# Interleaving two arrays: 64 KiB store rows from one output buffer, one DMA queue in a fixed order

## The chip, the cores and the metric

The kernel runs on one NeuronCore of a Trainium2 chip. The metric is the device time of one execution in microseconds; lower is better. The core has 16 DMA engines that move data between HBM (the chip's main memory) and SBUF (the core's working memory, 128 partitions). A DMA is issued by an engine's queue (here those of SyncE, called SP in the profile, and of ScalarE, called ACT), and a DMA over 128 partitions puts 8 partition rows on each of the 16 DMA engines.

## What is computed

Two float32 arrays of 32 x 256 x 1024 elements are interleaved element by element:

```python
result = np.zeros((batch, seq, dim * 2), dtype=np.float32)
result[..., 0::2] = x
result[..., 1::2] = y
```

There is no arithmetic. The kernel reads 67.11 MB and writes 67.11 MB.

## The kernel before

All of `x` is seen as one flat run and cut into `n` = 8 tiles. A tile is 128 partitions x `W` = 8192 elements, 4 MiB, so a row of one partition is 32 KiB of HBM in one piece. `y` is cut in the same way. A tile of the output is 128 x 16384 elements, 8 MiB, 64 KiB for each partition.

SBUF holds six buffers of 32 KiB a partition: `xt[0]`, `xt[1]` for tiles of x, `yt[0]`, `yt[1]` for tiles of y, and `ot[0]`, `ot[1]` for the two halves of an output tile. Tile k uses `xt[k % 2]` and `yt[k % 2]`; half h of its output always goes through `ot[h]`.

Three engines run lists written out by hand, and semaphores order them:

- SyncE issues the loads (lines 37 to 48). The first half of x tile 0 comes first; ScalarE issues the other half at line 38, and both are moved ahead of the start barrier by `tile_interleave_kernel`. Then come y0, x1 and y1, which wait for nothing. From k = 2 on, the load of x tile k (line 45) waits until VectorE has counted `woven` up to the last copy that reads that `xt` buffer, and the load of y tile k (line 48) waits for one copy more.
- VectorE weaves (lines 50 to 63). For each tile and each half h it copies 4096 elements of x into the even elements of `ot[h]` (line 60) and then 4096 elements of y into the odd ones (line 63). Each copy adds 1 to `woven`. The x copy waits for x and, from the second tile on, until the store that last read `ot[h]` has landed (`osem[h]`, line 59). The first y copy of a tile waits for y.
- ScalarE issues the stores (lines 65 to 70): for each half, when its two copies are done, one DMA of 128 rows of 32 KiB, 64 KiB apart in HBM.

At the end ScalarE waits for all stores of `ot[0]` and clears the semaphores, and SyncE waits for the last store of `ot[1]`.

Of the kernel before, what the change touches and what calls it, by code (L numbers as in the profile page):

```python
# [3 lines left out]


def _interleave(nc, x, y, out):
    P = 128
    W = 8192
    H = W // 2  # L10

    total = 1
    for s in x.shape:
        total *= s
    n = total // (P * W)
    assert n * P * W == total

    def rows(ap, names, k):
        flat = ap.rearrange("b s d -> (b s d)")
        return flat[k * names : (k + 1) * names].rearrange("(p w) -> p w", p=P)  # L20

    fp32 = mybir.dt.float32
    xt = [nc.alloc_sbuf_tensor(f"xt{b}", [P, W], fp32).ap() for b in (0, 1)]
    yt = [nc.alloc_sbuf_tensor(f"yt{b}", [P, W], fp32).ap() for b in (0, 1)]
    ot = [nc.alloc_sbuf_tensor(f"ot{b}", [P, W], fp32).ap() for b in (0, 1)]

    xsem = [nc.alloc_semaphore(f"xsem{b}") for b in (0, 1)]
    hsem = nc.alloc_semaphore("hsem")
    ysem = [nc.alloc_semaphore(f"ysem{b}") for b in (0, 1)]
    woven = nc.alloc_semaphore("woven")  # L30
    osem = [nc.alloc_semaphore(f"osem{b}") for b in (0, 1)]

    xs = [rows(x, P * W, k) for k in range(n)]
    ys = [rows(y, P * W, k) for k in range(n)]
    os_ = [rows(out, 2 * P * W, k) for k in range(n)]

    nc.sync.dma_start(out=xt[0][:, :H], in_=xs[0][:, :H]).then_inc(xsem[0], 16)
    nc.scalar.dma_start(out=xt[0][:, H:], in_=xs[0][:, H:]).then_inc(hsem, 16)

    for k in range(n):  # L40
        b = k % 2
        if k >= 2:
            nc.sync.wait_ge(woven, 4 * (k - 2) + 3)
        if k:
            nc.sync.dma_start(out=xt[b], in_=xs[k]).then_inc(xsem[b], 16)
        if k >= 2:
            nc.sync.wait_ge(woven, 4 * (k - 2) + 4)
        nc.sync.dma_start(out=yt[b], in_=ys[k]).then_inc(ysem[b], 16)

    for k in range(n):  # L50
        b = k % 2
        for h in (0, 1):
            c = slice(h * H, (h + 1) * H)
            if h == 0:
                nc.vector.wait_ge(xsem[b], 16 * (k // 2 + 1))
            elif k == 0:
                nc.vector.wait_ge(hsem, 16)
            if k:
                nc.vector.wait_ge(osem[h], 16 * k)
            nc.vector.tensor_copy(out=ot[h][:, 0::2], in_=xt[b][:, c]).then_inc(woven, 1)  # L60
            if h == 0:
                nc.vector.wait_ge(ysem[b], 16 * (k // 2 + 1))
            nc.vector.tensor_copy(out=ot[h][:, 1::2], in_=yt[b][:, c]).then_inc(woven, 1)  # L63

    for k in range(n):
        for h in (0, 1):
            nc.scalar.wait_ge(woven, 4 * k + 2 * h + 2)
            nc.scalar.dma_start(
                out=os_[k][:, h * W : (h + 1) * W], in_=ot[h]
            ).then_inc(osem[h], 16)  # L70

    nc.scalar.wait_ge(osem[0], 16 * n)
    used = sorted(s.num for s in [*xsem, hsem, *ysem, woven, osem[0]])
    assert used == list(range(used[0], used[-1] + 1)), used
    nc.scalar.sem_clear(range(used[0], used[-1] + 1))
    nc.sync.nop(nofuse=True).wait_op(osem[1], 16 * n, "sem-ge").then_inc(
        osem[1], -16 * n
    )


def kernel(tc, x, y, out):
    nc = tc.nc
    tc.close()
    tc.compile()

    _interleave(nc, x, y, out)

    blocks = nc.main_func.blocks
    for engine in (mybir.EngineType.SP, mybir.EngineType.Activation):
        opening = blocks[0].instructions  # L90
        at, moved = next(
            (b, i)
            for b in blocks[1:]
            for i in b.instructions
            if i.engine == engine and i.opcode == "DMACopy"
        )
        assert not (moved.sync_info and moved.sync_info.on_wait)
        body = at.instructions
        body.remove(moved)
        gate = next(  # L100
            n
            for n, i in enumerate(opening)
            if i.engine == engine and i.opcode == "Drain"
        )
        opening.insert(gate, moved)
        at.instructions = body
        blocks[0].instructions = opening


# [1 line left out]
_INS = ['x', 'y']  # L111
_OUTS = [((32, 256, 2048), 'float32')]


# [23 lines left out]
```

## Time and profile before

| | us |
|---|---|
| median of 8 runs | 314.64 (314.48 to 314.90) |
| the profiled execution | 314.74 |
| its span, first to last instruction | 313.4 |
| VectorE busy in the span | 72.6 (23%), 32 copies |

The profile is one execution. Two rows of the page's table of groups tell what VectorE waits for. After the bar stand the busy time, the mean duration of one copy in ns, the idle time of the engine just before these copies, and what ended it:

```profile
L60 DVE COPY ot<-xt 128x4096 f32<-128x4096 f32 x16 | 36.7, 2295 | 183.2 <-DMA out_dram<-ot 171.5
L63 DVE COPY ot<-yt 128x4096 f32<-128x4096 f32 x16 | 36.7, 2291 | 42.8 <-DMA yt<-in_y_dram 42.8
```

The DMAs by the place where they are issued: the number of them, the size of one, and the median time from issue to landing:

```profile
out_dram<-ot ACTq DMA_DIRECT2D x16, 4096.0 KB, 29.0
yt<-in_y_dram SPq DMA_DIRECT2D x8, 4096.0 KB, 60.8
xt<-in_x_dram SPq DMA_DIRECT2D x7, 4096.0 KB, 43.6
xt<-in_x_dram SPq DMA_DIRECT2D x1, 2048.0 KB, 11.7
xt<-in_x_dram ACTq DMA_DIRECT2D x1, 2048.0 KB, 13.4
```

q1 in the profile is SyncE's DMA queue and q10 is ScalarE's. A packet is what a DMA engine records of one row, or of the small write to a semaphore with which each DMA ends on each engine.

### The profile page before, as it was taken

Reading aid. Unit: us, or ns where it says so; the run is one execution under the profiler, and the core shown is the slowest. Engines: PE = TensorE matmul, PEld = TensorE weight load, DVE = VectorE, ACT = ScalarE, POOL = GpSimd, SP = SyncE. Lnnn points to the kernel's source line nnn. Section 1 sums busy time; section 2 is a strip of 40 time slices with the busy share of each in tenths; the row PEclk is TensorE's granted clock in tenths of the full one; section 3 lists DMA queues with packets and bytes.
Section 4 is the critical chain, followed back from the end, with each engine's and each line's share of the span. In section 5 each row is a group of like instructions: output and inputs, shape, how many; then the busy total and the mean of one; then the engine's idle time right before and its main releaser. Section 6 shows DMA issues by size and latency. Waiting matters only on the chain.

```text
span 313.4 us, 113 instructions
## 1 busy us (share of the span) xinstructions
DVE 72.6 (23%) x32; POOL 0.2 (0%) x4
## 2 busy tenths in 40 slices
DVE  0216002232022410324103250031501315013510
POOL 0000000000000000000000000000000000000000
DMA  8999999999999999999999999999999999999998
GB/s 339 464 406 397 431 439 427 443 418 452 410 460 406 460 406 460 410 456 414 447 422 439 431 435 435 431 439 422 447 414 456 406 460 406 460 410 456 414 452 351
DMA packets 4752, 134.22 MB, mean 428 GB/s; under 512 B 528, under 2 KB 528, under 8 KB 528
## 3 DMA queue, kind: packets, MB, share of 16 engines
q10 hardware_dynamic: 2448, 69.21, 51.2%
q1 hardware_dynamic: 2304, 65.01, 48.5%
HBM read 67.11 MB, written 67.11 MB: 428 GB/s over the span
## 4 chain that ended last, share of the span: by engine, by line
DMA 82%; DVE 12%; issue 0%
DMA out_dram<-ot 76%; DMA yt<-in_y_dram 7%; DVE ot L63 6%; DVE ot L60 6%
## 5 line engine op out<-in xcount | busy, mean ns | idle before, releaser
L60 DVE COPY ot<-xt 128x4096 f32<-128x4096 f32 x16 | 36.7, 2295 | 183.2 <-DMA out_dram<-ot 171.5
L63 DVE COPY ot<-yt 128x4096 f32<-128x4096 f32 x16 | 36.7, 2291 | 42.8 <-DMA yt<-in_y_dram 42.8
L122 POOL MEMSET const-uint8-127<- 128x1 uint8 x1 | 0.1, 103 | 0.0
L122 POOL MEMSET const-bfloat16-1.0<- 128x1 bf16 x1 | 0.1, 102 | 0.0
L122 POOL MEMSET const-float32-0.0<- 128x1 f32 x1 | 0.1, 99 | 0.2 <-issue 0.2
L122 POOL MEMSET const-float32-1.0<- 128x1 f32 x1 | 0.1, 99 | 0.0
## 6 DMA issues: line engine op xcount, KB each, us to landing
out_dram<-ot ACTq DMA_DIRECT2D x16, 4096.0 KB, 29.0
yt<-in_y_dram SPq DMA_DIRECT2D x8, 4096.0 KB, 60.8
xt<-in_x_dram SPq DMA_DIRECT2D x7, 4096.0 KB, 43.6
xt<-in_x_dram SPq DMA_DIRECT2D x1, 2048.0 KB, 11.7
xt<-in_x_dram ACTq DMA_DIRECT2D x1, 2048.0 KB, 13.4
```

Source lines behind the costliest of these rows:

```text
L60: nc.vector.tensor_copy(out=ot[h][:, 0::2], in_=xt[b][:, c]).then_inc(woven, 1)
L63: nc.vector.tensor_copy(out=ot[h][:, 1::2], in_=yt[b][:, c]).then_inc(woven, 1)
L122: nc = _bacc.Bacc("TRN2", target_bir_lowering=False, num_devices=1)
```

## The change

- The buffers are regrouped. `pair[0]` and `pair[1]` each hold a tile of x and a tile of y side by side (64 KiB a partition); `ot` is one output buffer of 64 KiB a partition. The bytes of SBUF are the same.
- An output tile is stored by one DMA with rows of 64 KiB, in place of two DMAs with rows of 32 KiB.
- SyncE issues everything but the second half of x tile 0, in this order: the loads of tiles 0 and 1, then for each k the store of tile k and the loads of tile k + 2. The one wait in the loop is for `woven` to reach the last copy of tile k.
- VectorE weaves a tile as two copies of x (both halves) and then two of y. From the second tile on it waits until the whole store of the tile before has landed, since there is one output buffer.
- The last tile is not woven into `ot` but into `pair[0]`, whose tile 6 has been woven by then. It waits for the copies of tile 6 (`woven`) and for its own loads, and not for a store. Its store has a semaphore of its own, `last`.
- SyncE clears the semaphores and waits for the last store.

```diff
--- before.py
+++ after.py
@@ -20,15 +20,17 @@
         return flat[k * names : (k + 1) * names].rearrange("(p w) -> p w", p=P)
 
     fp32 = mybir.dt.float32
-    xt = [nc.alloc_sbuf_tensor(f"xt{b}", [P, W], fp32).ap() for b in (0, 1)]
-    yt = [nc.alloc_sbuf_tensor(f"yt{b}", [P, W], fp32).ap() for b in (0, 1)]
-    ot = [nc.alloc_sbuf_tensor(f"ot{b}", [P, W], fp32).ap() for b in (0, 1)]
+    pair = [nc.alloc_sbuf_tensor(f"pair{b}", [P, 2 * W], fp32).ap() for b in (0, 1)]
+    xt = [p[:, :W] for p in pair]
+    yt = [p[:, W:] for p in pair]
+    ot = nc.alloc_sbuf_tensor("ot", [P, 2 * W], fp32).ap()
 
     xsem = [nc.alloc_semaphore(f"xsem{b}") for b in (0, 1)]
     hsem = nc.alloc_semaphore("hsem")
     ysem = [nc.alloc_semaphore(f"ysem{b}") for b in (0, 1)]
     woven = nc.alloc_semaphore("woven")
-    osem = [nc.alloc_semaphore(f"osem{b}") for b in (0, 1)]
+    osem = nc.alloc_semaphore("osem")
+    last = nc.alloc_semaphore("last")
 
     xs = [rows(x, P * W, k) for k in range(n)]
     ys = [rows(y, P * W, k) for k in range(n)]
@@ -37,45 +39,47 @@
     nc.sync.dma_start(out=xt[0][:, :H], in_=xs[0][:, :H]).then_inc(xsem[0], 16)
     nc.scalar.dma_start(out=xt[0][:, H:], in_=xs[0][:, H:]).then_inc(hsem, 16)
 
-    for k in range(n):
+    def load(k):
         b = k % 2
-        if k >= 2:
-            nc.sync.wait_ge(woven, 4 * (k - 2) + 3)
         if k:
             nc.sync.dma_start(out=xt[b], in_=xs[k]).then_inc(xsem[b], 16)
-        if k >= 2:
-            nc.sync.wait_ge(woven, 4 * (k - 2) + 4)
         nc.sync.dma_start(out=yt[b], in_=ys[k]).then_inc(ysem[b], 16)
+
+    load(0)
+    load(1)
+    for k in range(n):
+        nc.sync.wait_ge(woven, 4 * k + 4)
+        src = ot if k < n - 1 else pair[n % 2]
+        nc.sync.dma_start(out=os_[k], in_=src).then_inc(
+            osem if k < n - 1 else last, 16
+        )
+        if k + 2 < n:
+            load(k + 2)
 
     for k in range(n):
         b = k % 2
-        for h in (0, 1):
-            c = slice(h * H, (h + 1) * H)
-            if h == 0:
-                nc.vector.wait_ge(xsem[b], 16 * (k // 2 + 1))
-            elif k == 0:
-                nc.vector.wait_ge(hsem, 16)
-            if k:
-                nc.vector.wait_ge(osem[h], 16 * k)
-            nc.vector.tensor_copy(out=ot[h][:, 0::2], in_=xt[b][:, c]).then_inc(woven, 1)
-            if h == 0:
+        dst = ot if k < n - 1 else pair[n % 2]
+        nc.vector.wait_ge(xsem[b], 16 * (k // 2 + 1))
+        if k == 0:
+            nc.vector.wait_ge(hsem, 16)
+        elif k < n - 1:
+            nc.vector.wait_ge(osem, 16 * k)
+        else:
+            nc.vector.wait_ge(woven, 4 * k)
+        for first, half in ((0, xt[b]), (1, yt[b])):
+            if first:
                 nc.vector.wait_ge(ysem[b], 16 * (k // 2 + 1))
-            nc.vector.tensor_copy(out=ot[h][:, 1::2], in_=yt[b][:, c]).then_inc(woven, 1)
+            for h in (0, 1):
+                nc.vector.tensor_copy(
+                    out=dst[:, 2 * h * H + first : 2 * (h + 1) * H : 2],
+                    in_=half[:, h * H : (h + 1) * H],
+                ).then_inc(woven, 1)
 
-    for k in range(n):
-        for h in (0, 1):
-            nc.scalar.wait_ge(woven, 4 * k + 2 * h + 2)
-            nc.scalar.dma_start(
-                out=os_[k][:, h * W : (h + 1) * W], in_=ot[h]
-            ).then_inc(osem[h], 16)
-
-    nc.scalar.wait_ge(osem[0], 16 * n)
-    used = sorted(s.num for s in [*xsem, hsem, *ysem, woven, osem[0]])
+    nc.sync.wait_ge(osem, 16 * (n - 1))
+    used = sorted(s.num for s in [*xsem, hsem, *ysem, osem, woven])
     assert used == list(range(used[0], used[-1] + 1)), used
-    nc.scalar.sem_clear(range(used[0], used[-1] + 1))
-    nc.sync.nop(nofuse=True).wait_op(osem[1], 16 * n, "sem-ge").then_inc(
-        osem[1], -16 * n
-    )
+    nc.sync.sem_clear(range(used[0], used[-1] + 1))
+    nc.sync.nop(nofuse=True).wait_op(last, 16, "sem-ge").then_inc(last, -16)
 
 
 def tile_interleave_kernel(tc, x, y, out):
```

More of the change, by code (lines that the diff above doesn't have):

```diff
@@ L38, in _interleave @@
     nc.scalar.dma_start(out=xt[0][:, H:], in_=xs[0][:, H:]).then_inc(hsem, 16)
+    def load(k):
+        b = k % 2
+        if k:
+            nc.sync.dma_start(out=xt[b], in_=xs[k]).then_inc(xsem[b], 16)
+        nc.sync.dma_start(out=yt[b], in_=ys[k]).then_inc(ysem[b], 16)
+    load(0)
[8 more added lines that the diff above has]
+            load(k + 2)
@@ L40, in _interleave @@
     for k in range(n):
         b = k % 2
-        if k >= 2:
-            nc.sync.wait_ge(woven, 4 * (k - 2) + 3)
-        if k:
-            nc.sync.dma_start(out=xt[b], in_=xs[k]).then_inc(xsem[b], 16)
-        if k >= 2:
-            nc.sync.wait_ge(woven, 4 * (k - 2) + 4)
-        nc.sync.dma_start(out=yt[b], in_=ys[k]).then_inc(ysem[b], 16)
-    for k in range(n):
-        b = k % 2
-        for h in (0, 1):
-            c = slice(h * H, (h + 1) * H)
-            if h == 0:
-                nc.vector.wait_ge(xsem[b], 16 * (k // 2 + 1))
-            elif k == 0:
-                nc.vector.wait_ge(hsem, 16)
-            if k:
-                nc.vector.wait_ge(osem[h], 16 * k)
-            nc.vector.tensor_copy(out=ot[h][:, 0::2], in_=xt[b][:, c]).then_inc(woven, 1)
-            if h == 0:
-                nc.vector.wait_ge(ysem[b], 16 * (k // 2 + 1))
-            nc.vector.tensor_copy(out=ot[h][:, 1::2], in_=yt[b][:, c]).then_inc(woven, 1)
```

## The prediction, made before the run

> **What bounds the kernel now.** I read the page first: how full are the DMA engines, and who waits for them?
>
> ```profile
> span 313.4 us, 113 instructions
> ...
> DVE 72.6 (23%) x32; POOL 0.2 (0%) x4
> ...
> DMA  8999999999999999999999999999999999999998
> ...
> DMA packets 4752, 134.22 MB, mean 428 GB/s; under 512 B 528, under 2 KB 528, under 8 KB 528
> ...
> DMA 82%; DVE 12%; issue 0%
> ```
>
> VectorE works 23% of the span; the 16 DMA engines are full in 38 of 40 slices. The 12% of DVE in the chain is not exposed time: the DMA row shows no hole under those pieces. So ask not who waits, but what keeps 134.22 MB from moving faster. The timeline gives the rate of the middle (start, duration, line):
>
> ```profile
> 106.47 2.30 DVE L60 COPY ot<-xt 128x4096 f32<-128x4096 f32 x1 [9.77 <-DMA out_dram<-ot]
> ...
> 145.20 2.30 DVE L60 COPY ot<-xt 128x4096 f32<-128x4096 f32 x1 [9.79 <-DMA out_dram<-ot]
> ```
>
> One tile takes 145.20 - 106.47 = 38.73 us and moves 16.78 MB: 433 GB/s. Eight tiles at that pace are 309.8 us of the 313.4. The rest, 3.6 us, must lie at the ends or in one place. Windows of 20 us (DVE time, POOL time, clock, DMA share, GB/s last) find a place:
>
> ```profile
> 4.00:24.00 20.00, 4.29 (x2) 0.00 (x0) 1.00 1.03 443
> 24.00:44.00 20.00, 4.71 (x3) 0.00 (x0) 1.00 0.99 410
> 44.00:64.00 20.00, 4.59 (x2) 0.00 (x0) 1.00 1.01 434
> ```
>
> A window counts a packet where it starts, which blurs a single one, so I summed the trace's records of single packets (queue, size, start, duration). Against a steady 433.2 GB/s the transfers are 2.0 us late after start-up, still 2.0 at 26 us, and 2.9 from 30 us to the end. So 0.89 us is lost once, between 26 and 30 us. That is where the first store (issued 24.34) joins a stream of loads: load packets of 1,213 ns stretch to as much as 2,095 ns just ahead of the first store packet at 29.24. After that, load and store packets alternate on every engine, each again at 1,213 ns, with nothing lost.
>
> The tail has stores alone. In the chain the store released at 265.89 lands at 294.02:
>
> ```profile
> 265.89 28.13 DMA out_dram<-ot
> ```
>
> The two stores left land by 313.4: 9.7 us for each 4.19 MB, again 433 GB/s. Loads alone, stores alone and a mixture all run at one rate, the engines'.
>
> **The packets, where the gain is.** The packet records give three durations: 611 ns for 16 KiB, 1,213 ns for 32 KiB, 9 ns for the small packet that ends each DMA on each engine (33 DMAs x 16 engines = the 528 packets under 512 B). Another 16 KiB costs 602 ns, so 9 ns of each data packet is fixed. A 64 KiB row should take 9 + 4 x 602 = 2,417 ns in place of 2 x 1,213 = 2,426. An engine stores 8 rows of each of 8 tiles: 64 x 9 ns = 0.58 us saved. DMAs fall from 33 to 25: 8 x 9 ns = 0.07 us. Together 0.65 us.
>
> The timeline gives less. Without any fixed cost an engine's 32 data packets of a tile are 32 x 1,204 ns = 38.53 us; the tile takes 38.73, so 0.20 us is spread over 32 + 4 packets, 5.6 ns each. Dropping 9 of 36 packets a tile saves 8 x 9 x 5.6 ns = 0.40 us. I take 0.5, between two measures of one thing. No 64 KiB packet is in the trace; should such a row travel as two pieces, only the 0.07 is left.
>
> A rule of the Trainium skill ("DMA: Bandwidth & Descriptors", section "Why small descriptors are slow") sizes the fixed cost smaller: about 3 cycles for each packet. By its 850 MHz that would be 3.5 ns, and the saving about 0.25 us, an estimate from that page; no run here shows those cycles.
>
> **Woven tiles and waits.** VectorE keeps 32 copies of 2.29 us, x halves first. Tile 0 then waits for ScalarE's half as well (issued 0.12, landed about 13.5), weaves x until 18, waits for y0 (22.0) and finishes at 26.5 in place of 28.7. SyncE's queue now holds x1 and y1 until 22.0 + 2 x 9.68 = 41.4 us, so store 0, issued at 26.6, stands 15 us behind work.
>
> With one output buffer the weave of tile k waits for the whole of store k-1; the x copy, the y copies, and SyncE's wait for `woven`, with store k and the two loads of tile k+2 behind it, stand behind that. The ring meanwhile holds x(k+1) and y(k+1), 19.4 us; the weave is 4 x 2.25 = 9.0 us. Store 0 ends at 60.8, the weave of tile 1 at 69.8, the loads of tile 2 at 80.1: 10.3 us of cover in each tile. If the cover were gone, up to 9 us a tile would lie open.
>
> The last tile needs the freed pair for that reason: no loads follow it, and in the one buffer its weave would wait for store 6 and expose about 9 us. Woven into pair 0 it starts when tile 6 is done. Its y lands when store 6 begins, two copies (4.6 us) follow, and store 7 is queued 14.8 us before store 6 ends. Nothing opens.
>
> SyncE issues 24 DMAs in place of 16 at 0.33 to 0.45 us each; its queue is 10 us ahead, so that costs nothing. ScalarE keeps one. The clearing of the semaphores moves to SyncE, under store 7, as it stood under the last store before: nothing.
>
> **One queue, two directions.** Before, on each engine a ring of stores lay beside a ring of loads; now 8 MB runs of loads and stores follow one another in one ring. Rows of before: y0 to x1 on SyncE's ring, and three stores in a row on ScalarE's, go on at full pace over the DMA boundary. A turn inside one ring, load to store or back, is not shown. Its nearest rows disagree: packets that alternate between rings turn every 1.2 us for nothing; the first store cost 0.89 us. A turn therefore costs between 0 and 0.89 us, or less than nothing in that the single 0.89 may go. I take the many free turns, with the first-store loss kept once.
>
> A rule speaks against the change here: "Perfetto Trace Analysis", section "DMA Instruction — HWDGE (DVE, Sync)", says that a DMA's last descriptor, the semaphore's, waits until its write is confirmed, "a surprisingly long delay especially when the write target is HBM". Loads queued behind each store would wait for it if it held the ring. The tail speaks against that: a store's semaphore packet lies between the last stores, and they keep 9.7 us each.
>
> **Sum.** The profiled execution took 314.74 us, 1.3 more than its span; the median of the runs is 314.64, 0.10 lower. Minus 0.5 and plus nothing else gives a profiled 314.24 and a median of 314.1.
>
> **Rivals.**
> - *The first-store loss goes too.* If the 0.89 us belongs to a second ring that wakes beside a busy one, a single ring never pays it: 314.64 - 0.5 - 0.89 = 313.25. For: store 0 now lies in the ring 15 us before its turn. Against: ScalarE's ring had worked until 13.5 us already, and then the x0 halves interleaved with no such stretch after the cold start.
> - *Every turn from loads to stores pays it* (the slower side). Eight turns in place of one: 7 x 0.89 - 0.5 = +5.7, 320.4 us. For: the only change from pure loads to stores in the trace lost 0.89, in packets of loads ahead of it. Against: the mixture turns all the time for nothing, and the change from mixture to stores alone at 288 us lost nothing. From 0.25 us a turn on (8 x 0.25 - 0.89 - 0.5 = +0.6) it decides the sign.
> - *The rows are cut.* A 64 KiB row runs as two packets: 314.64 - 0.07 = 314.6. For: no packet over 32 KiB is in the trace. Against: every row so far was one packet, whatever its size.
>
> **How the numbers follow.** A measurement of this kernel can tell about 0.2%, 0.63 us, from no change. My forecast, turns free and the loss kept once, gets 0.35; its own range is 313.9 to 314.3, and with its two packet measures 0.40 and 0.65 it just touches the limit, so 0.04 of it counts as faster. The lost first-store loss gets 0.31, turns that cost 0.25 us or more 0.28, cut rows 0.06. Faster: 0.31 + 0.04 = 0.35. Same: 0.31 + 0.06 = 0.37. Slower: 0.28. The low end is the first rival with the larger packet saving: 314.64 - 0.89 - 0.65 = 313.1, with 0.1 for the runs' scatter 313.0. At the top I take in turns up to about 0.53 us: 8 x 0.53 - 0.89 - 0.5 = +2.9, 317.5, some 0.12 of the 0.28; about 0.16 is left out above.
>
> **What would show it.** In the profile after, one queue carries nearly all, packets fall to 128 x (2 + 7 + 8 + 8) + 25 x 16 = 3,600, store packets last 2,417 ns, the tile period is 38.65 to 38.68 us, and VectorE's y copies of a middle tile end about 10 us before that store's first packet. The late time in the packet sums stays at 2.9 us (forecast), near 2.0 (first rival), or climbs with each tile (second). I am wrong if a hole of DMA stands at a turn, if loads are long behind each store, or if a VectorE wait ends after the ring has run empty.

## The result, and the profile after

The changed kernel is slower: a median of 317.23 us (316.43 to 317.83, 10 runs) against 314.64. The ratio is 1.0079, with a 95% interval of 1.0071 to 1.0087: 2.6 us lost where 0.5 us was to be gained. On three other occasions, each on a chip of its own, it took 315.25, 315.42 and 315.24 us (ratios 1.0028, 1.0036 and 1.0028 to the kernel before on the same chip, intervals 1.0012 to 1.0052 taken together). So it is slower each time, by an amount that differs from occasion to occasion; whether that lies in the chip or in chance is not shown. On each of these three chips its executions range over more than 2 us (314.64 to 317.13 on one of them), where the kernel before stays mostly within 0.5. That scatter is part of the finding.

The profiled execution after took 316.74 us, 2.0 more than the one before. Its page:

```profile
span 315.4 us, 106 instructions
...
DVE 71.4 (23%) x32; POOL 0.2 (0%) x4
...
DMA  8999999999999999999999999999999989999995
...
DMA packets 3600, 134.22 MB, mean 426 GB/s; under 512 B 400, under 2 KB 400, under 8 KB 400
...
q1 hardware_dynamic: 3456, 132.12, 97.6%
...
DMA 71%; DVE 17%; SPq 0%; issue 0%; DVEq 0%
```

The change did what it says: 3,600 packets, nearly all on SyncE's queue (q1). The DMA row is still full but for an 8 near 256 us and the last slice, 5 where it was 8. A packet counts where it starts, and packets of 64 KiB blur that row, so it is a hint only. The timeline gives the tile period (start and duration of the four copies of a tile):

```profile
61.97 8.90 DVE L73 COPY ot<-pair 128x4096 f32<-128x4096 f32 x4 [35.49 <-DMA out_dram<-ot]
100.77 8.90 DVE L73 COPY ot<-pair 128x4096 f32<-128x4096 f32 x4 [29.90 <-DMA out_dram<-ot]
139.83 8.90 DVE L73 COPY ot<-pair 128x4096 f32<-128x4096 f32 x4 [30.15 <-DMA out_dram<-ot]
179.02 8.90 DVE L73 COPY ot<-pair 128x4096 f32<-128x4096 f32 x4 [30.29 <-DMA out_dram<-ot]
217.76 8.90 DVE L73 COPY ot<-pair 128x4096 f32<-128x4096 f32 x4 [29.84 <-DMA out_dram<-ot]
257.45 8.90 DVE L73 COPY ot<-pair 128x4096 f32<-128x4096 f32 x4 [30.79 <-DMA out_dram<-ot]
```

From start to start: 38.80, 39.06, 39.19, 38.74, 39.69 us. The forecast was 38.65 to 38.68; before it was 38.71 to 38.74. A steady machine would repeat one number. This one loses a different amount in each tile.

A store has landed when all 16 DMA engines have written their rows. The landings of the last store, engine by engine, tell the story (us; taken from the trace's records of the semaphore that each DMA engine raises):

| | first engine | median | last engine |
|---|---|---|---|
| before | 312.80 | 313.07 | 313.39 |
| after | 312.59 | 313.12 | 315.37 |

The quickest engine got faster by 0.2 us, the median one stayed where it was, and the last came 2.0 us later. That is the whole loss: four of the 16 engines fall behind (their landings are at 314.71 and later, the other twelve at 313.82 or earlier), and the kernel ends with the slowest. The spread of a store's 16 landings grows along the run: 0.63 us for store 0, then 0.73, 1.03, 1.54, 1.47, 2.68, 2.78, 2.77. In the profiles of the changed kernel on the three other chips the time follows this spread too: 315.24 us with a last spread of 1.37 us, 316.24 with 2.34, 316.71 with 2.93, while the median landing stays between 312.87 and 313.05.

Where they fall behind is in the packet records. A 32 KiB load takes 1,213 ns and a 64 KiB store 2,418. After the start-up nearly all that is longer lies at turns from loads to stores, in the last loads of an engine before its first store packet. Such a longer packet is called stretched below. Over the 16 engines, the first turn (at 38 to 41 us) costs 0.88 us on average, as the one join cost 0.86 before (the place where the first store comes in beside the loads of the other queue). There are seven turns, not eight as the prediction and the expectations count, since no load stands between stores 6 and 7. The six later turns together cost 0.73 us on average (before: 0.00), very unevenly: at the turn near 235 us ten packets are stretched, the longest by 0.99 us.

### The profile page after: what moved, and what is told of

The parts are those of the page before. It is cut to its first block, busy times and chain, and to the rows that moved or that the text cites. A ratio compares the mean times of both kernels' runs of the same rounds, so it can differ in the third digit from the quotient of the medians.

```text
span 315.4 us, 106 instructions
## 1 busy us (share of the span) xinstructions
DVE 71.4 (23%) x32; POOL 0.2 (0%) x4
## 4 chain that ended last, share of the span: by engine, by line
DMA 71%; DVE 17%; SPq 0%; issue 0%; DVEq 0%
DMA out_dram<-ot 49%; DMA pair<-in_y_dram 22%; DVE ot L73 16%; DVE pair L73 1%; SPq L45 0%; SPq L53 0%; DVEq L66 0%
## 5 line engine op out<-in xcount | busy, mean ns | idle before, releaser
L73 DVE COPY ot<-pair 128x4096 f32<-128x4096 f32 x28 | 62.4, 2290 | 203.9 <-DMA out_dram<-ot 186.5
L73 DVE COPY pair<-pair 128x4096 f32<-128x4096 f32 x4 | 9.0, 2292 | 5.9 <-DMA pair<-in_y_dram 5.2
```

What stands on the lines that cost most here:

```text
L73: nc.vector.tensor_copy(out=dst[:, 2 * h * H + first : 2 * (h + 1) * H : 2], in_=half[:, h * H : (h + 1) * H],).then_inc(woven, 1)
```

## The experiments

The diffs are shortened: `...` and comment lines stand for code that is not printed. A ring is the list of one queue's packets on one DMA engine; the spread is that of a store's 16 landings, for the last store where no other is named.

The theories, as the expectations call them. T: each turn from loads alone to stores stretches the last loads of some engines, and an engine that falls behind does not catch up. Q: the single ring is at fault. R: the 64 KiB rows are. Later L: stores issued late into a busy ring.

**Stores on ScalarE's queue again** (one output buffer and 64 KiB rows kept).

```diff
-        nc.sync.wait_ge(woven, 4 * k + 4)
-        nc.sync.dma_start(out=os_[k], in_=src).then_inc(...)
+        nc.scalar.wait_ge(woven, 4 * k + 4)
+        nc.scalar.dma_start(out=os_[k], in_=src).then_inc(...)
+        # SyncE: x of tile k+2 at woven 4k+2, y at woven 4k+4
```

> Changed kernel with its 64 KiB-row stores issued by ScalarE again (own ring); x of tile k+2 is loaded as soon as its x buffer is woven, 4.5 us earlier than y. One output buffer stays, so each 9 us weave is a stretch of loads alone, and each store then joins it: eight joins as before, but in two rings. Theory T (each time stores follow a stretch of pure loads, the last load packets of some engines stretch, and engines that fall behind never catch up): nothing gained, 316.5 to 318, last store's 16 landings spread over 1.5 us or more, stretched load packets of 1.3 to 2.2 us ahead of each store. Rival Q (the single ring is the cause: two rings interleave and level the engines): about 314.1 to 314.4, spread about 0.6 us, one loss of 0.9 us only. Rival R (64 KiB rows are the cause): 316.5 to 317.5, as T.

Measured: a median of 334.23 us, with six executions from 327.4 to 339.1; the two quickest, 327.4 and 331.6, give a ratio of 1.0474 (1.0422 to 1.0527). No theory had this. Windows of the slowest execution, the profiled one (DVE time, POOL, clock, DMA share, GB/s), show the DMA engines running dry:

```profile
150.00:165.00 15.00, 8.90 (x4) 0.00 (x0) 1.00 0.85 354
195.00:205.00 10.00, 3.41 (x2) 0.00 (x0) 1.00 0.54 229
```

In this execution the 16 landings of the load of x tile 5 are spread over 21.8 us, and those of store 3 over 3.9 us (197.64 to 201.50). The weave of tile 4 waits for the last of these:

```profile
201.59 8.90 DVE L77 COPY ot<-pair 128x4096 f32<-128x4096 f32 x4 [37.74 <-DMA out_dram<-ot]
```

With one output buffer there is nothing to store until it is done, and from 202 to 207 us 14 of the 16 engines have no load left either. In this kernel a second ring did not level the engines. Because of the holes this run can't separate T from Q.

**32 KiB rows, one ring.** Each store of the changed kernel becomes two DMAs.

```diff
-        nc.sync.dma_start(out=os_[k], in_=src)...
+        for h in (0, 1):
+            c = slice(h * W, (h + 1) * W)
+            nc.sync.dma_start(out=os_[k][:, c], in_=src[:, c])...
```

> Changed kernel with each tile's store split into two DMAs with rows of 32 KiB, back to back on SyncE's queue; order and buffers unchanged. Theory T (turns from loads to stores): the loss stays and the packet saving goes, 317.2 + 0.5 = 317.7 (317.0 to 318.4), landings of the last store spread over 1.5 to 3.5 us. Rival Q (single ring): the same. Rival R (long 64 KiB packets hold up the loads beside them): back to 314.6 to 315.2 with a spread of 0.6 us.

316.22 us, ratio 1.0050 (1.0035 to 1.0065), spread of the last landings 1.84 us. R alone is out: with 32 KiB rows the kernel is still slower than before, and its landings are still spread three times as far (0.59 us before). Against the 317.23 of the first measurement the long rows seemed to cost 1 us; the repeat at the end shows that times from two occasions can't be compared so.

**Kernel before, all in one ring, runs of 4 MB.**

```diff
+        nc.sync.wait_ge(woven, 4 * k + 2 * h + 2)
+        nc.sync.dma_start(out=os_[k][:, h * W : (h + 1) * W], in_=ot[h])...
+        if k + 2 < n:   # x after half 0, y after half 1
+            nc.sync.wait_ge(woven, 4 * k + 3 + h)
+            nc.sync.dma_start(out=t, in_=v[k + 2])...
```

> Kernel before (two output halves, 32 KiB rows) with all DMAs but the second half of x0 on SyncE's queue, as half store, x load, half store, y load: runs of 4 MB in one ring, 14 turns from loads to stores in place of 7 or 8. Theory T: each turn after the first costs the slowest engine about as much as in the changed kernel (2.6 + 0.5 = 3.1 us over 7 turns, 0.44 each), so 13 x 0.44 = 5.8 us: about 320.4, and at least 318; spread of the last landings 3 us or more. Rival Q with no role for the number of turns: 317 to 318. Rival R: 314.6.

318.38 us, ratio 1.0113 (1.0098 to 1.0127), 2.2 us above the 8 MB runs with the same rows on the same chip. The landings are spread over 3.78 us: first engine 313.25, median 313.37, last 317.03. The bound of 318 holds, the 320.4 does not: the cost for each turn is less than I took (there are 13 turns, not 14). By the time alone the 317 to 318 of Q is not excluded, since the interval reaches down to 317.6; that more turns cost more rests on the comparison on one chip. Note the median: most engines lose almost nothing.

**An early small store in the kernel before.**

```diff
+    nc.vector.memset(ot[0][:, :128], 0.0).then_inc(early, 1)
+    nc.scalar.wait_ge(early, 1)
+    nc.scalar.dma_start(out=os_[0][:, :128], in_=ot[0][:, :128]).then_inc(esem, 16)
+    nc.vector.wait_ge(esem, 16)
```

> Kernel before with one extra store of 64 KB in all (128 rows of 512 bytes of zeros, later overwritten by the first store) issued by ScalarE within the first microseconds; it leaves nothing out. It tests what the single loss of 0.89 us at the first store is. If it is a first-write effect: the stretch at 26 to 30 us goes, 314.64 - 0.89 + about 0.1 for the small store = 313.85. Theory T (it is the turn from loads alone to stores, whoever wrote before): the stretch stays where it was, 314.6 to 314.9.

314.89 us, ratio 1.0017 (1.0005 to 1.0029). The stretch is there, 0.79 us, around 30 us, with another 0.21 us at 55 to 65 us; it moved because the first weave had to wait until the small store landed at 23.4. So the join's loss is no first-write effect. The packet records show one thing more: from 14 to 21.6 us the small store's packets (512 bytes, 27 ns each) alternate with loads on every engine, and the loads keep their 1,213 ns. Not every store that comes in beside loads stretches them.

**The changed kernel again, and one turn only.** These three and the next one ran on one chip. In the two kernels with one turn all loads come first:

```diff
+    for k in range(2, n):
+        nc.sync.wait_ge(woven, 4)
+        nc.sync.wait_ge(ysem[k % 2], 16 * (k // 2))
+        load(k)
+    for k in range(n):
+        nc.sync.dma_start(out=os_[k], in_=ot)...      # or two DMAs, 32 KiB rows
```

> The changed kernel itself, beside the others of this call on one chip. 317.2 (316.4 to 317.9), last store's landings spread over 2 to 3 us.

> One queue, same loads and same 64 KiB-row stores, but all eight tiles are loaded first and then eight stores follow: one turn from loads to stores in place of eight. It weaves only tile 0 and stores it eight times, so tiles 1 to 7 are left out of the output. Theory T (the price is at the turns, and 64 KiB packets by themselves save 9 ns each): the loss of 0.9 us once, then 314.6 - 0.5 = 314.1 (313.9 to 314.4), landings spread 0.6 us. Rival R (64 KiB packets are dearer by themselves, turn or no turn): 315 or more with a spread above 1.5 us. Rival Q (any long work in a single ring drifts): 315 or more.

> As the kernel with one turn and 64 KiB rows (it too weaves only tile 0 and leaves tiles 1 to 7 out of the output), but each store is two DMAs with 32 KiB rows. Theory T: 314.6, spread 0.6 us, 0.4 to 0.65 us above its 64 KiB twin. Rival R: 314.6, below its twin. Rival Q: 315 or more, like its twin.

Changed again: 315.25 us. One turn: 313.80 us with 64 KiB rows (ratio 0.9978, 0.9969 to 0.9987) and 314.16 with 32 KiB (0.9985, 0.9976 to 0.9993), both with landings spread over 0.51 us. Three things follow. A single ring does not drift by itself, so Q is out. 64 KiB rows save 0.36 us, so R is out once more and the packet step of the prediction stands. And the one turn, at 157 us, cost 0.00 and 0.04 us in place of 0.8, which the expectations did not have. The page of the version with 32 KiB rows, for the last slices:

```profile
DMA  8999999999999999999999999999999999999998
GB/s 341 463 406 461 406 452 419 444 427 423 448 411 457 406 452 419 436 436 415 457 402 465 406 452 419 444 427 444 427 419 452 406 465 402 465 406 457 415 444 360
```

and of the version with 4 MB runs, with the same row size:

```profile
DMA  8999999999999999999999999999999999999995
GB/s 341 453 438 422 405 405 446 430 430 438 422 455 405 459 409 451 413 446 426 434 434 426 446 409 455 413 446 418 434 438 418 451 413 459 401 459 397 463 397 227
```

Between them the rows are alike until the last slice, 360 against 227 GB/s: there some engines have finished and wait for others.

**16 KiB rows, one ring.** The loop above with four DMAs a tile.

> Changed kernel with each tile's store cut into four DMAs with 16 KiB rows, order unchanged: eight turns in one ring. Against the version with 32 KiB rows (316.2) an engine has 128 more data packets, 0.7 to 1.2 us. If a turn costs the less the shorter the store's packets are (64 KiB rows 317.2, 32 KiB 316.2), the 1.7 us that the 32 KiB version loses against the kernel before halve: 316.3, spread about 1 us. If the turn does not depend on the row: 317.2, spread 1.8 us as with 32 KiB.

318.63 us (ratio 1.0136, 1.0119 to 1.0153), spread 3.29 us: worse than either forecast. Later turns cost 0.88 us on average. Short rows make a turn no cheaper.

**The order without the weave, an early first store, other addresses.** All on one chip, with the changed kernel beside them.

```diff
+    for what, k in [("S", 0), ("L", 2), ("S", 1), ("L", 3), ...]:
+        if what == "L":
+            nc.sync.wait_ge(ysem[k % 2], 16 * (k // 2))
+            load(k)
+        else:   # every store sends ot
+            nc.sync.dma_start(out=os_[k], in_=ot)...
```

The second kernel has this loop over store 0, loads 2 to 7, stores 1 to 7. The third is the changed kernel with `os_[(k + 4) % n]` for `os_[k]`.

> The changed kernel once more, as the yardstick of this call's chip: 314.7 to 317.8; its landings are spread over 1 to 3 us whenever it is above 315.

> The changed kernel's DMAs in exactly its order and sizes, eight turns, but every store sends the woven tile 0, so that nothing waits for a weave (tiles 1 to 7 are left out of the output) and each DMA is issued some 40 us before its turn in place of 10. Theory T (the turns themselves stretch loads): as the changed kernel in this call, 315 to 317, stretched load packets ahead of the stores, the first one by 0.8 us. Rival L (a store that is issued late into a ring that loads keep busy does it; with DMAs issued long before, the turn is free as it was with one turn): 313.8, no stretch, spread 0.6 us.

> One queue: loads of tiles 0 and 1, store 0, loads of tiles 2 to 7, then seven stores; every store sends the woven tile 0 (tiles 1 to 7 are left out of the output). The first turn is at 41 us and its store is issued at 26.5 us as in the changed kernel; the second, at about 177 us, is issued long before. If the first store after loads always costs 0.8 us: 313.8 + 0.8 = 314.6, stretch at 38 to 41 us. If it cost nothing with one turn because it was issued long before (rival L): the stretch at 38 to 41 us is there too (issued late), none at 177, 314.6. If the one turn was free because no loads stood behind the store: stretch at the first, none at the second. If neither shows a stretch, 313.8, the weave's traffic or the late waits are at fault.

> The changed kernel with store k sent to the place of tile (k + 4) mod 8 of the output (the output's halves are exchanged): the same order and waits, other HBM addresses of the stores beside those of the loads. If the stretch comes from addresses of loads and stores that disturb each other in HBM: another size of it at each turn, perhaps none, 314.0 to 314.5 or well above the changed kernel. Theory T and rival L: no difference from the changed kernel in this call.

| | us | ratio (interval) | first turn, mean loss | later turns, mean loss | spread |
|---|---|---|---|---|---|
| changed again | 315.42 | 1.0036 (1.0020 to 1.0052) | 0.90 | 0.14 | 1.37 |
| its order, no weave | 316.01 | 1.0041 (1.0028 to 1.0055) | 0.94 | 0.48 | 1.40 |
| store 0 early, two turns | 314.62 | 1.0004 (0.9995 to 1.0012) | 0.78 | 0.00 | 0.57 |
| stores elsewhere | 316.45 | 1.0058 (1.0041 to 1.0074) | 0.97 | 0.32 | 2.93 |

The order alone, without any weave to wait for and with all DMAs behind the first store issued long ahead, is as slow as the changed kernel. So the output buffer and the waits for it are not the cause, and L is out. Two turns in place of seven, on the same chip, are level with the kernel before. With other addresses the stretch stays; the interval overlaps that of the changed kernel, so nothing is shown there.

**Why the first turn costs, and how many turns it takes.** On one chip again, three kernels without the weave:

```diff
+    # loads 0-3, store 0, loads 4-7, stores 1-7      first turn at 80 us
+    # loads 0-1, stores 0-3, loads 2-7, stores 4-7   four stores behind the first turn
+    # loads 0-1, stores 0-1, loads 2-3, ...          four turns, 16 MB runs
```

> One queue, 64 KiB rows, every store sends the woven tile 0 (tiles 1 to 7 are left out of the output): loads of tiles 0 to 3, store 0, loads of tiles 4 to 7, seven stores. Two turns, the first at about 80 us with loads behind it. If a turn is dear because loads stand behind the store: a stretch of 0.8 us at 78 us, 314.6. If it is dear because it comes early in the run: no stretch, 313.8.

> One queue, 64 KiB rows, woven tile 0 in every store (tiles 1 to 7 are left out of the output): loads of tiles 0 and 1, four stores, loads of tiles 2 to 7, four stores. The first turn is at 41 us with 77 us of stores behind it. If early turns are dear: a stretch of 0.8 us at 38 us, 314.6. If only loads close behind make it dear: none, 313.8.

> As the order without the weave (every store sends tile 0, tiles 1 to 7 are left out of the output), but two tiles of loads and two stores alternate: four turns. Two turns took 314.62, eight took 316.01: 0.23 us for each turn after the first. If the number of turns sets the loss: 314.6 + 2 x 0.23 = 315.1 (314.7 to 315.6), landings spread about 1 us. If each engine's loss came with the time in one queue and not with turns: 316.

| | us | ratio (interval) | first turn, mean loss | later turns | spread |
|---|---|---|---|---|---|
| first turn at 80 us | 314.25 | 0.9990 (0.9981 to 0.9999) | 0.63 | 0.00 | 0.67 |
| four stores behind it | 314.76 | 1.0009 (0.9999 to 1.0018) | 0.97 | 0.00 | 0.74 |
| four turns | 314.73 | 1.0011 (1.0003 to 1.0020) | 0.80 | 0.05 | 0.81 |

Both simple readings of the first turn fall: at 80 us it costs 0.63, between the 0.7 to 1.0 at 41 us and the nothing at 157; and with 77 us of stores behind it, it costs no less. It fades the later it comes, and why stays open. The length of the loads ahead of it does not settle it: in the version with the first turn at 80 us the second turn comes after as long a run of loads (78 us) and costs 0.00. The free turn at 157 us is not all gain: in the two versions with one turn, most load packets take 1,218 ns in place of 1,213 from about 40 us on, and the transfers fall 0.3 to 0.4 us further behind before the turn comes. In the version with four turns the three later ones cost 0.05 us together, so the loss does not grow evenly with their number: with runs of 8 MB (seven turns) it begins, with runs of 4 MB it is worse. Number and length of the runs change together here, and no version parts them.

**The kernel before with an earlier start.**

```diff
-    nc.scalar.dma_start(out=xt[0][:, H:], in_=xs[0][:, H:]).then_inc(hsem, 16)
+    nc.scalar.dma_start(out=yt[0][:, :H], in_=ys[0][:, :H]).then_inc(hsem, 16)
+    nc.sync.dma_start(out=xt[0][:, H:], in_=xs[0][:, H:]).then_inc(xh, 16)
```

> Kernel before, complete, with another start: ScalarE's first DMA is the first half of y0 in place of the second half of x0, and SyncE loads x0 and y0 in halves, so the first store is issued at about 16 us in place of 24.3 and joins the loads at about 19. If the join costs 0.86 us whenever it comes: 314.5. If it is cheaper the fewer loads went before: down to 313.8.

314.86 us, ratio 1.0011 (1.0002 to 1.0020): the join costs 1.05 us at 16 to 24 us. No version of the whole kernel beat the one before.

**The rows once more, on one chip.**

> Changed kernel with 32 KiB store rows in one queue, beside the changed kernel on one chip. If rows act as they do with one turn (64 KiB rows save 0.36 us) and turns cost the same for both: 0.4 us above the changed kernel. If long rows make a turn dearer: up to 1 us below it.

> The changed kernel on the same chip, as the yardstick: 315.2 to 317.3.

32 KiB rows 316.95 (ratio 1.0066, 1.0044 to 1.0089), 64 KiB rows 315.24 (1.0028, 1.0013 to 1.0044). The medians are 1.7 us apart, the expectations had 0.4 above or up to 1 below, and the intervals only touch. Within the changed kernel the long rows don't hurt; if anything they help by more than the 0.36 us of the pair with one turn.

## Why the prediction was wrong, point by point

- **What bounds the kernel** was right: the DMA engines, full in both kernels until their last packets.
- **The packets** were right in kind and a little large. 2,418 ns for a 64 KiB row were measured, 2,417 worked out. I took 0.5 us between 0.40 and 0.65; the pair with one turn gives 0.36. That is 72 packets of an engine saved (64 rows and 8 small ones), 5.0 ns each: nearer to the 5.6 of the tile period than to the 9 of the single packet, and above the about 3 cycles (by the prediction's estimate 3.5 ns) of the Trainium skill's "DMA: Bandwidth & Descriptors", section "Why small descriptors are slow".
- **The weave, the single output buffer and the freed pair** cost nothing, as said: the order without the weave is no faster.
- **The semaphore behind each store** did not hold the ring, as the tail had suggested: loads followed a store in the kernels with two and four turns, and there the later turns together lost 0.05 us at most.
- **The turns** are the step that failed. I bounded a turn in one ring between 0 and 0.89 us, saw that its nearest rows disagreed, and took "the many free turns, with the first-store loss kept once". The second half was right (0.88 us, once). The first was not: six later turns cost 0.73 us on average in the profiled execution, more than the whole saving, and the engine that ended last lost more still (next point). The late time of the packet sums, the prediction's own sign, stands at 2.9 us after the first turn and at 3.4 at 240 us. Packets that alternate between two rings were a poor neighbour for a turn inside one; that this is so because no run of loads ends there is my reading, not a test. That the first-store loss would be kept came out, but partly by luck: the kernels with one turn show that it can be nothing.
- **The sum was over the wrong engine.** I added up one engine as if it stood for 16. That held before, where nothing happened after 30 us and the landings ended within 0.59 us. It fails as soon as a cost is uneven: the median engine lost its saving to the turns and came out level, and the last engine set the time, 2.0 us later. In the versions with one queue a spread of more than 1 us never shrank by more than 0.5 us again. In versions with two queues it did: from 3.14 us at 59 us to 0.67 at 62 in the kernel before with the earlier start, and from 21.8 to 0.2 in the one with holes. Whether lost time was made up there, or only the order of the two rings' packets changed, is not shown.
- **The second rival** (every turn pays) had the right sign and place. Its count is one too high: seven turns in place of one make 6 x 0.89 - 0.5 = +4.8 us and not +5.7, and the sign turns at 0.29 us a turn and not at 0.25. What the last engine paid is just above that: the spread grew from 0.63 to 2.77 us over six turns, 0.36 each. Its price of 0.89 for each was too high, and the top of the range, worked out with eight turns of 0.53, has the same slip. The first rival (the first-store loss goes) is refuted by 0.88 us in the changed kernel; the third (rows cut) by the 2,418 ns packets.

What stays open: the mechanism. The records show that the stretched packets are an engine's last loads, and that at several turns the engines that turn last lose most (near 118 us those whose last load began in the 0.7 us before another engine's first store lost 0.21 to 0.47 us, the earlier ones 0 to 0.24). That would make laggards lag more, as seen: followed from packet to packet, the four engines whose first packet of store 1 came last, 0.8 to 1.0 us behind the quickest, are the four last at store 5, by 2.2 to 2.8 us. It was read from the records, not tested: no kernel here holds the engines level, and none delays a single one. Nor is it shown whether as many turns would cost as much with loads and stores in two queues, since the one kernel that tried it ran dry.

## What to carry to other kernels

Where DMA is the bound, the end is the slowest DMA engine's: read a transfer's 16 landings, not its last one alone, and watch whether their spread grows along the run. A steady mixture of loads and stores from two queues kept 16 engines together for 280 us here; runs of 8 MB of loads and stores in turn saved packets, and some engines fell behind, while two to four turns in all cost little beyond the first. When two neighbouring rows disagree on a price that is paid many times, keep the dear one in the forecast until the row nearest in kind, here the one join on record, is explained.

## What the runs showed of the hardware

- A row of 64 KiB moves as one packet of 2,418 ns; 64 KiB rows in place of 32 KiB saved 0.36 us of 314, no more.
- The first turn from loads alone to stores with rows of 16 to 64 KiB, or the join, cost 1.05 us at 16 to 24 us, 0.7 to 1.0 at 26 to 42, 0.63 at 80 and nothing at 157 us. Later turns cost 0.05 us or less together with two or four turns in one queue, and 0.14 to 0.88 us with seven.
- A DMA's engines finish on their own, as the Trainium skill's "DMA: Bandwidth & Descriptors" says in the section "Why a DMA increments its semaphore by 16 and not by 1"; here that was 2.8 us from first to last in one ring, and 21.8 us in two rings with one output buffer.
- A small store of 64 KB, issued at 1.9 us behind ScalarE's half of x0 (landed at 13.5) and beside SyncE's loads, landed at 23.4 us: its eight short packets on an engine took turns with loads of 1,213 ns.
- One and the same kernel had medians of 317.23, 315.25, 315.42 and 315.24 us on four occasions, while the kernel before stayed between 314.47 and 314.64. A kernel whose time scatters so must be compared with others on one chip and at one time.
